# First mixture's weights in runs of 4 KB, and RWKV keys with the learning-rate factor left in PSUM

## The chip, the cores and the metric

One NeuronCore of a Trainium2 chip runs the whole program. The metric is the time of one execution on the device in microseconds. The kernel before took 2755.37 us (median of 3 runs, 2753.96 to 2766.93).

The engines: TensorE multiplies matrices (weights loaded first, then a matmul that streams the other operand) and writes to PSUM; VectorE, ScalarE and GpSimd work element by element, each on 128 partitions; the first two read and write SBUF and PSUM, GpSimd SBUF only. SyncE here only issues DMAs, in order, each behind a wait for what it needs. Every engine runs its own instructions in order.

## The reference

Two layers over 512 latent and 256 context tokens of 1024 channels, fp32. Layer 0 mixes tokens by neighbourhood attention, layer 1 by a bidirectional RWKV-7 scan; each is followed by a mixture of 16 experts in which every expert takes the 64 latent (in layer 0 also the 32 context) tokens with the highest affinity.

```
y   = segment_sum(((silu(xin @ w1) * (xin @ w3)) @ w2) * gate)      # per expert: [cap,1024] x [1024,1024], three times
kk  = k * k_k ; kk = kk / max(norm(kk per head), 1e-12)               # k = xk @ w_k
a_z = sigmoid(a0_z + (xa @ a1_z) @ a2_z)                              # learning rate, z = forward, backward
scan inputs: kk, kk * a_z, kt_z = k * (1 + (a_z - 1) * k_a), decay from w0, w1, w2
bonus = sum over z of sum per head(r * kt_z * r_k)
```

## The kernel before, in words

**Mixture.** For each expert twelve weight tiles of 1 MB ([128, 2, 1024] fp32) go through a ring of SBUF buffers (`load_weights`, L637): eight of `w1` and `w3` by turns, four of `w2`. A tile holds 256 rows of the matrix; partition p has rows 2p and 2p+1, one run of 8 KB (`"(p k) n -> p k n"`, L645). So a tile's half k holds every second row, and the activations that multiply it have to hold every second channel. `pair_cols` (L69) picks these columns when activations are turned with a transpose on TensorE (`transpose`, L75 to L77: the data is loaded as weights, the identity is multiplied): gathered tokens `xg` in `channels` (L659; used by `gather` and, for the router, by `route_tile` on `XN`), and the hidden rows `hid` and `hidc` in `expert` (L805, L814). The norm's gain, the adaLN columns and the router weights follow the same order of channels (`load_vectors`, `ada`, `moe_open`). TensorE computes `P` (L790, latent) and `Pc` (L795, context), then `w2` (L823, L828). A weight DMA is issued on SyncE's queue once TensorE has done with the tile that its buffer held.

**Keys.** `rw_inputs` weaves the products of layer 1 (`w_r`, `w_k`: L260 to L262, three passes per product) with `rw_keys`, which goes over four blocks of 256 channels (n), each in six steps of 128 tokens (t). `norms` multiplies k by `k_k` on GpSimd for a pair of steps (L1199), squares on ScalarE and sums on VectorE. `weights` loads two rows of vectors (`krows`, one buffer: the DMA waits until GpSimd has done with the block before) and the LoRA matrices, and splits these in high and low parts `w2s` and `w`. A step has three parts. `first`: GpSimd multiplies k by `k_k` again (`kkb`, L1232) and by half of `k_a` (`kr`, L1234); TensorE makes two PSUM tiles `mk` (L1241, L1242; three buffers), ScalarE takes tanh of them into SBUF, `sig` for the decay and `av` for the learning rate (L1243). `second`: `kkb` is normalised on VectorE (L1250), ScalarE makes `hk` from it, and VectorE makes `kka` (L1257) and in two operations the new `av` (L1259, L1260) from the factor; all go to DRAM (`pkd`). `third` (latent steps, four a block): GpSimd's three products and VectorE's sum `cf` for the bonus. After the last block come the value products (`xvh`, `xvl` from `xraw`; weights `w_v`, of which `wh` is made on ScalarE at L252 and `wl` on VectorE at L253).

**Order.** Each engine's order is made when the program is built, by a list scheduler that goes by simulated times and the priorities that the code gives. So an edit in one place can move instructions of others, on every engine and on the DMA queues.

Of the kernel before, what the change touches and what calls it, by code (L numbers as in the profile page):

```python
# [31 lines left out]
P = 128  # L32
# [36 lines left out]
def pair_cols(k):  # L69

    o = 2 * P * (k // 2)
    return slice(o + k % 2, o + 2 * P, 2)
# [7 lines left out]
def load_vectors(S):  # L80


    nc, cp, I = S.nc, S.cp, S.I
    cr = S.small.tile([16, P], F32, name="crows", bufs=1)
    nc.sync.dma_start(cr[0:8], I["c"].rearrange("o (k p) -> (o k) p", p=P))
    nc.sync.dma_start(cr[8:16], I["c_ctx"].rearrange("(k p) -> k p", p=P))
    S.sT = cp.tile([P, KD, 32], F32, name="sT")
    nc.vector.memset(S.sT, 0.0)
    pt = S.ps_tp.tile([P, 512], F32, name="tp")
    transpose(S, pt[:, :16], cr)  # L90
    nc.scalar.activation(S.sT[:, :, 0:2].rearrange("p k w -> p w k"),
                         pt[:, 0:16].rearrange("p (w k) -> p w k", w=2), AF.Silu)
    rows = S.small.tile([18, P], F32, name="rows", bufs=1)
    rows2 = S.small.tile([8, 2 * P], F32, name="rows2", bufs=1)
    q = nc.gpsimd
    q.dma_start(rows[0:16], I["norm1_g"].rearrange("l (k p) -> (l k) p", p=P))
    q.dma_start(rows2, I["norm2_g"].rearrange("l (k c) -> (l k) c", c=2 * P))
# [4 lines left out]
    transpose(S, pt[:, :18], rows)  # L102
    for s in range(2):
        transpose(S, pt[:, 18 + 8 * s:26 + 8 * s], rows2[:, s::2])
    S.vT = cp.tile([P, 34], F32, name="vT")
    nc.vector.tensor_copy(S.vT[:, 0:18], pt[:, 0:18])
    nc.vector.tensor_copy(S.vT[:, 18:34].rearrange("p (k s) -> p s k", s=2),
                          pt[:, 18:34].rearrange("p (s k) -> p s k", s=2))
    S.g1T = [S.vT[:, 8 * l:8 + 8 * l] for l in range(2)]
    S.g2T = [S.vT[:, 18 + 8 * l:26 + 8 * l] for l in range(2)]  # L110
    S.qgT = cp.tile([P, 1], F32, name="qgT")
    nc.vector.tensor_scalar(S.qgT, S.vT[:, 16:17], DH ** -0.5, None, op0=ALU.mult)
    S.kgT = S.vT[:, 17:18]
    S.modT = [cp.tile([P, 48, 2], F32, name=f"modT{l}") for l in range(2)]


def ada(S, l, j):
# [22 lines left out]
    for s in range(2):  # L140
        transpose(S, pt[:, s, :], acc[:, s::2] if j in (3, 4) else acc[:, s * P:(s + 1) * P])
# [459 lines left out]
def moe_open(S, l, es):  # L601
# [9 lines left out]
    if WRING[l][0]:  # L611
# [3 lines left out]
    nc.gpsimd.dma_start(R.wr.rearrange("p (k s) e -> p k (s e)", s=2),  # L615
                        I["moe_router"][l].rearrange("(k p s) e -> p k (s e)", p=P, s=2))
# [42 lines left out]
def channels(S, rows):  # L659
# [11 lines left out]
def route_tile(S, R, t):  # L671
# [14 lines left out]
    modulated(S, R, channels(S, XN), t // NLT, hT)  # L686
# [81 lines left out]
def gather(S, R, i, w):  # L768
# [3 lines left out]
    modulated(S, R, channels(S, xg), w, xin)  # L772
# [3 lines left out]
def expert(S, R, e, xin, xinc, wk, psh, Y, YC):  # L776
# [27 lines left out]
    for c in range(4):  # L804
        transpose(S, pt[:, c * P:(c + 1) * P], hid[:, pair_cols(c)])  # L805
    hT = wk.tile([P, 4, 2, CAPL], F32, name="hidT")
    nc.scalar.activation(hT.rearrange("p c h s -> p (c h s)"), pt, AF.Copy)  # L807
    if ctxs:
# [4 lines left out]
        for c in range(4):  # L813
            transpose(S, pt[:, c * 64:(c + 1) * 64], hc[0:64, pair_cols(c)])  # L814
# [350 lines left out]
SPREAD, LOQ, KSB, BOOST = 8, 7, 6, 1000  # L1165
# [7 lines left out]
def rw_keys(S, ready):  # L1173
# [15 lines left out]
    def norms(n, C):  # L1189
# [3 lines left out]
        C.ss = kp.tile([P, NT, 4], F32, name="kss")  # L1193
        for t in range(0, NT, 2):
# [751 lines left out]
```

## Time and profile before

| | |
|---|---|
| profiled execution | 2758.18 us |
| its span | 2756.4 us |
| TensorE busy | 2470.2 us (90%) |
| VectorE, ScalarE, GpSimd busy | 1327.1, 1004.0, 591.5 us |
| DMA | 637.64 MB, mean 231 GB/s |
| weight tiles of the mixtures | 378 on SyncE's queue, 6 on GpSimd's, 1024 KB each |

The span is the time from the first to the last instruction of the profiled execution, the rest of its own time lies around it. An instruction is named by its line in the program, engine, and out<-in by the program's names. A busy TensorE need not be at its peak: its clock is granted in two levels (1.2 and 2.4 GHz; 1.00 is the higher). "a <- b" in a list of waits says that a stood idle until b was done. Stages follow one another: attention to 640 us, the first mixture to 1283, RWKV inputs to 1388, keys to 1523, their tail to 1571, values and scan to 2232, and the second mixture.

### The profile page before, as it was taken

To read this page: it belongs to the slowest core of one execution; us is meant where nothing else is said; L and a number is where in the kernel's file an instruction comes from. 1 tells how busy PE (TensorE), PEld (TensorE's weight loads), DVE (VectorE), ACT (ScalarE), POOL (GpSimd) and SP (SyncE) were. 2 spreads that over 40 slices of the span, in tenths; PEclk is the share of its full clock that TensorE was granted. 3 is DMA by queue.
4 is the path that set the end of the run, shared out by engine and by line. 5 is a ranking of instruction groups with operands and counts; after the bars stand their busy time and mean duration, and the time that the engine had idled before them with its cause. 6 is when DMAs were issued, how large, how long until landed. Compare 5 with 4: busy or idle time off the path is not lost. (4 is left out here: it accounts for less than half of the span.)

```text
span 2756.4 us, 44025 instructions
## 1 busy us (share of the span) xinstructions
PE 2470.2 (90%) x16800; PEld 1574.1 (57%) x16800; DVE 1327.1 (48%) x3006; ACT 1004.0 (36%) x2127; POOL 591.5 (21%) x857
## 2 busy tenths in 40 slices
PE   6998999898999999997698697999999977998887
PEld 4876879793333333333388686777777862332222
DVE  6665566642222222225978845666666771221222
ACT  3555556642111101113266634766665431000100
POOL 2100000121000000001656525665655110000000
PEclk9999999998999999998899898999999978999999
DMA  8646440328787878784157866565554369999998
GB/s 246 147 150 187 132 152 15 109 100 327 298 320 312 334 305 329 293 357 172 69 186 241 269 167 130 124 134 125 126 122 125 87 243 378 420 420 421 420 420 342
DMA packets 378371, 637.64 MB, mean 231 GB/s; under 512 B 133832, under 2 KB 301056, under 8 KB 329008
## 3 DMA queue, kind: packets, MB, share of 16 engines
q1 hardware_dynamic: 370944, 609.11, 63.5%
q0 software_dynamic: 7216, 25.70, 2.5%
q8 instruction: 134, 2.20, 0.3%
q14 instruction: 77, 0.63, 0.1%
HBM read 565.11 MB, written 53.88 MB: 225 GB/s over the span
## 5 line engine op out<-in xcount | busy, mean ns | idle before, releaser
L790 PE MATMUL P<-wm,xin 128*64 128x512 f32 x2048 | 494.3, 601 | 25.8 <-DMA wm<-in_moe_w_dram 24.7
L790 PEld LDWEIGHTS P<-wm,xin 128*64 128x64 f32 x2048 | 141.0, 137 | 328.3 <-issue 259.4
L823 PE MATMUL mm<-wm,hidT 128*64 128x512 f32 x1024 | 245.9, 601 | 16.8 <-ACT hidT L807 14.9
L801 ACT ACTIVATE hid<-P 128x512 f32<-128x512 f32 x32 | 19.1, 597 | 563.3 <-PE P L790 563.3
L763 POOL DMA_INDIRECT xg<-xnd,ii x20 | 19.7, 985 | 846.5 <-PE tp L77 571.5
L837 DVE SCALAR_TENSOR_TENSOR Y<-mm,gates,gt 64x512 f32<-64x512 f32 x64 | 48.0, 750 | 283.1 <-PE mm L823 282.4
L260 PE MATMUL mm<-wh,hTh 128*128 128x256 f32 x576 | 173.5, 302 | 1.9 <-ACT hTh L554 1.9
L802 DVE TENSOR_TENSOR hid<-P,hid 128x512 f32<-128x512 f32 x32 | 22.1, 692 | 308.3 <-PE P L790 293.6
L262 PE MATMUL mm<-wh,hTl 128*128 128x256 f32 x576 | 168.4, 293 | 1.9 <-DVE hTl L557 1.9
L261 PE MATMUL mm<-wl,hTh 128*128 128x256 f32 x576 | 168.7, 293 | 0.0
L823 PEld LDWEIGHTS mm<-wm,hidT 128*64 128x64 f32 x1024 | 72.7, 137 | 151.9 <-issue 121.3
L1477 POOL TENSOR_TENSOR Wi<-Wi,Ti 112x30 f32<-112x30 f32 (+14 forms) x240 | 141.4, 589 | 18.8
L1475 POOL TENSOR_TENSOR Ti<-Wi 112x30 f32<-112x30 f32 (+14 forms) x240 | 134.9, 562 | 18.2
L795 PE MATMUL Pc<-wm,xin 128*32 128x512 f32 x1024 | 138.5, 597 | 0.0
L260 PEld LDWEIGHTS mm<-wh,hTh 128*128 128x128 f32 x576 | 114.3, 199 | 11.9 <-issue 8.8
L262 PEld LDWEIGHTS mm<-wh,hTl 128*128 128x128 f32 x576 | 113.6, 198 | 4.5 <-DVE hTl L557 2.8
L1554 PE MATMUL mm<-FR,QF 128*128 128x128 f32 (+1 forms) x768 | 115.1, 294 | 0.4 <-ACT QF L1542 0.4
L261 PEld LDWEIGHTS mm<-wl,hTh 128*128 128x128 f32 x576 | 114.6, 199 | 1.3 <-issue 1.1
L864 DVE TENSOR_TENSOR X<-mm,X 128x512 f32<-128x512 f32 x80 | 52.6, 687 | 111.9 <-PE mm L863 111.7
L1554 PEld LDWEIGHTS mm<-FR,QF 128*128 128x128 f32 x768 | 98.7, 200 | 7.4 <-ACT QF L1542 0.9
L1542 ACT ACTIVATE QF<-mm 64x256 f32<-64x256 f32 x192 | 72.6, 378 | 67.7 <-PE mm L1538 64.3
L1557 DVE TENSOR_TENSOR FT<-mm,eye 64x128 f32<-64x128 f32 x192 | 55.8, 292 | 78.9 <-ACT FT L1556 76.6
(437 smaller groups left out, 5715.6 us busy)
## 6 DMA issues: line engine op xcount, KB each, us to landing
wm<-in_moe_w_dram SPq DMA_DIRECT2D x378, 1024.0 KB
adaw<-in_ada_w_dram SPq DMA_DIRECT2D x96, 512.0 KB
wraw<-in_na_w_qkv_dram SPq DMA_DIRECT2D x32, 256.0 KB
wm<-in_moe_w_dram POOLq DMA_DIRECT2D x6, 1024.0 KB, 10.8
pkd<-sig SPq DMA_DIRECT2D x24, 256.0 KB
pkd<-kka SPq DMA_DIRECT2D x24, 256.0 KB
pkd<-av SPq DMA_DIRECT2D x24, 256.0 KB
sig<-pkd SPq DMA_DIRECT2D x16, 384.0 KB
```

Of the source, the lines that this page charges most:

```text
L260: S.nc.tensor.matmul(ps, xh, wh, start=(k == 0), stop=False)
L261: S.nc.tensor.matmul(ps, xh, wl, start=False, stop=False)
L262: S.nc.tensor.matmul(ps, xl, wh, start=False, stop=(k == n - 1))
L790: nc.tensor.matmul(ps[64 * hf:64 * hf + 64], xin[:, k, cl], w[:, hf * 512:(hf + 1) * 512], start=k == 0, stop=k == KD - 1)
L795: nc.tensor.matmul(Pc[32 * i:32 * i + 32], xinc[:, k, cc], ws[k][i // 2][:, (i % 2) * 512:(i % 2 + 1) * 512], start=k == 0, stop=k == KD - 1)
L823: nc.tensor.matmul(py[64 * hf:64 * hf + 64], hT[:, k % 4, k // 4, :], ws[k][:, hf * 512:(hf + 1) * 512], start=k == 0, stop=k == KD - 1)
L864: nc.vector.tensor_tensor(X[t][:, sl], ps, X[t][:, sl], op=ALU.add)
L1475: nc.gpsimd.tensor_tensor(t, W3[:, i + 1:32, i:i + 1].to_broadcast([112, n, i]), W3[:, i:i + 1, 0:i].to_broadcast([112, n, i]), op=ALU.mult)
L1477: nc.gpsimd.tensor_tensor(W3[:, i + 1:32, 0:i], W3[:, i + 1:32, 0:i], t, op=ALU.add)
L1542: nc.scalar.activation(QF[m][0:64, u], pq[64 * u:64 * u + 64], AF.Copy)
L1554: nc.tensor.matmul(pf[:, h, s0:], QF[m][:, u, h, :], rhs, start=True, stop=True)
L1557: nc.vector.tensor_tensor(F[64:128, :, 64:128], pf[64:128, :, 64:128], S.eye2[64:128, None, :].to_broadcast([64, 2, 64]), op=ALU.add)
```

## The change

In layer 0 alone, a weight tile's half k holds 128 neighbouring rows, so that each partition reads two runs of 4 KB; transposes, gain, adaLN columns and router weights of layer 0 go by neighbouring columns too. The second mixture stays with 8 KB. In the keys, `k * k_k` is made once for a pair of steps (`kkp`, four buffers, also the squares' source), and the learning-rate factor's tanh stays in its PSUM tile, from which VectorE's three operations read it; the last writes `av` to SBUF.

```diff
-def pair_cols(k):
+def block_cols(l, k):
+    if l == 0:
+        return slice(k * P, (k + 1) * P)
     o = 2 * P * (k // 2)
     return slice(o + k % 2, o + 2 * P, 2)
...
-    ...rearrange("(p k) n -> p k n", p=P))
+    ...rearrange(("(k p) n -> p k n", "(p k) n -> p k n")[R.l], p=P))
...
-            transpose(S, pt[:, i, :], rows[:, pair_cols(k)])
+            transpose(S, pt[:, i, :], rows[:, block_cols(l, k)])
...
-        transpose(S, pt[:, c * P:(c + 1) * P], hid[:, pair_cols(c)])
+        transpose(S, pt[:, c * P:(c + 1) * P], hid[:, block_cols(R.l, c)])
...
+            C.kp.append(kp.tile([P, 2, 256], F32, name="kkp", bufs=KPB))
+            q.tensor_tensor(C.kp[-1], k, both(C.kk), op=ALU.mult)
             sq = kp.tile([P, 2, 256], F32, name="kka")
-            q.tensor_tensor(sq, k, both(C.kk), op=ALU.mult)
-            nc.scalar.activation(sq, sq, AF.Square)
+            nc.scalar.activation(sq, C.kp[-1], AF.Square)
...
-        T.kk = kp.tile([P, 256], F32, name="kkb")
-        q.tensor_tensor(T.kk, T.k, C.kk, op=ALU.mult)
+        T.kk = C.kp[t // 2][:, t % 2, :]
...
-        T.av = kp.tile([P, 2, 256], F32, name="av", bufs=3)
-        for hid, i, dst in zip(S.hid, (0, 2), (T.sig, T.av)):
-            ps = S.ps_k.tile([P, 2, 256], F32, name="mk")
+        for hid, i in zip(S.hid, (0, 2)):
+            T.pa = ps = S.ps_k.tile([P, 2, 256], F32, name="mk")
...
-            nc.scalar.activation(dst, ps, AF.Tanh, scale=0.5)
+            nc.scalar.activation(ps if i else T.sig, ps, AF.Tanh, scale=0.5)
...
+        T.av = av = kp.tile([P, 2, 256], F32, name="av")
...
-        nc.vector.scalar_tensor_tensor(kka, av, 1.0, both(hk), op0=ALU.add, op1=ALU.mult)
+        nc.vector.scalar_tensor_tensor(kka, pa, 1.0, both(hk), op0=ALU.add, op1=ALU.mult)
...
-        nc.vector.scalar_tensor_tensor(av, av, -1.0, both(T.kr), op0=ALU.add, op1=ALU.mult)
-        nc.vector.tensor_tensor(av, av, both(T.k), op=ALU.add)
+        nc.vector.scalar_tensor_tensor(pa, pa, -1.0, both(T.kr), op0=ALU.add, op1=ALU.mult)
+        nc.vector.tensor_tensor(av, pa, both(T.k), op=ALU.add)
```

The order moves with it. SyncE's queue at the keys' tail, before (`r`, `av` and `krows` belong to the keys, `xraw` are the inputs of the value products; line numbers are each kernel's own):

```order
L1265 DMA r<-rd_10635 128x256
L955 DMA xraw<-xmd_10648 128x770
L955 DMA xraw<-xmd_10649 128x770
L955 DMA xraw<-xmd_10650 128x770
L955 DMA xraw<-xmd_10651 128x770
L955 DMA xraw<-xmd_10652 128x770
L955 DMA xraw<-xmd_10653 128x770
L955 DMA xraw<-xmd_10654 128x770
L955 DMA xraw<-xmd_10655 128x770
L1261 DMA pkd_10658<-av 128x2x256
L1170 DMA krows<-in_rw_k_a_dram 128x256
L1170 DMA krows<-in_rw_r_k_dram 128x256
```

The same place now:

```order
L1273 DMA r<-rd_10636 128x256 x2
L1177 DMA krows<-in_rw_k_a_dram 128x256
L1177 DMA krows<-in_rw_r_k_dram 128x256
L1269 DMA pkd_10659<-av 128x2x256
L1263 DMA pkd_10659<-sig 128x2x256
L962 DMA xraw<-xmd_10649 128x770
L962 DMA xraw<-xmd_10650 128x770
L962 DMA xraw<-xmd_10651 128x770
L962 DMA xraw<-xmd_10652 128x770
L962 DMA xraw<-xmd_10653 128x770
```

The last block's `krows` now go ahead of the eight `xraw`, which stand behind a store of `av` and one of `sig`.

TensorE in the last block, the second pair of `mk` tiles of a step before (`hs` and `h` are the LoRA activations of either direction, the last two numbers apart):

```order
L1241 MATMUL mk<-w2s,hs_10731 128x256 [waits Activation_49]
L1242 MATMUL mk<-w_13031,h_10732 128x256
L1241 MATMUL mk<-w2s,hs_10733 128x256
L1242 MATMUL mk<-w_13031,h_10734 128x256
L1241 MATMUL mk<-w2s,hs_10727 128x256 [waits Activation_49]
```

The same place now:

```order
L1248 MATMUL mk<-w2s,hs_10732 128x256 [waits DVE_49]
L1249 MATMUL mk<-w_13007,h_10733 128x256
L1248 MATMUL mk<-w2s,hs_10734 128x256
L1249 MATMUL mk<-w_13007,h_10735 128x256
L1248 MATMUL mk<-w2s,hs_10728 128x256 [waits Activation_49]
```

The first matmul into a reused `mk` tile waited for ScalarE and now, in 21 groups of the program (2 before), for VectorE.

## Rows read from the trace of the kernel before

**Rows 1.** The page's view of stages, asked for four stretches (first mixture, keys, keys' tail, second mixture): start and end in us, length, busy us and number of instructions of TensorE (PE), its weight loads (PEld), VectorE (DVE), ScalarE (ACT) and GpSimd (POOL), the granted TensorE clock, the DMA engines' busy share, GB/s.

```profile
640.00:1283.00 643.00, 632.42 (x3937) 224.71 (x3933) 143.44 (x246) 80.78 (x175) 10.44 (x15) 1.00 0.78 316
1388.00:1523.00 135.00, 124.39 (x998) 122.16 (x996) 103.60 (x126) 89.05 (x154) 83.65 (x82) 0.97 0.70 221
1523.00:1571.00 48.00, 25.24 (x131) 21.73 (x130) 41.55 (x54) 30.81 (x50) 29.27 (x30) 0.72 0.89 292
2310.00:2757.00 447.00, 391.49 (x1708) 136.31 (x1704) 97.70 (x162) 38.35 (x75) 5.62 (x6) 0.99 0.98 408
```

**Rows 2.** Who waited for whom, TensorE in the first mixture (640 to 1283 us), longest in total first: us in total, times, longest.

```profile
PE mm L823 <- ACT hidT L807: 7.9, 11, 0.7
```

**Rows 3.** The same for SyncE's DMA queue, same stretch.

```profile
SPq L645 <- PE Pc L795: 335.9, 75, 40.3
```

**Rows 4.** Stages again: two stretches with the DMA engines full, one where nearly all runs are of 4 KB (adaLN and attention weights), one where the weights of the first mixture come in 8 KB runs.

```profile
12.00:16.00 4.00, 2.09 (x16) 0.43 (x16) 0.75 (x2) 3.07 (x6) 0.00 (x0) 1.00 1.01 367
640.00:704.00 64.00, 62.63 (x372) 18.47 (x370) 6.18 (x10) 8.13 (x16) 1.97 (x2) 1.00 1.01 419
```

**Rows 5.** Transposes (L77), the weight loads: name, number, shortest/median/longest in ns, first and last start in us, shapes. `sb` is read in neighbouring columns, `xg` in every second one.

```profile
L77 PEld LDWEIGHTS tp<-ident,sb x320: 137/140/231, 101.5 to 530.2; 128*128 128x128 f32 x160
...
L77 PEld LDWEIGHTS tp<-ident,xg x160: 193/208/227, 634.5 to 2677.6; 128*128 128x128 f32 x160
```

**Rows 6.** TensorE in order of time, in the attention, around a block of four transposes of neighbouring columns: start in us, us, line, operation, number merged.

```profile
107.62 0.66 PE L77 MATMUL tp<-ident,sb 128*128 128x128 f32 x4
108.21 0.66 PE L406 MATMUL po<-PT,V 128*64 128x128 f32 x8
```

**Rows 7.** The same in the first mixture, around a block of four transposes of every second column.

```profile
713.89 0.75 PE L77 MATMUL tp<-ident,xg 128*128 128x128 f32 x4
714.57 0.65 PE L790 MATMUL P<-wm,xin 128*64 128x512 f32 x2
```

**Rows 8.** Who waited for whom, TensorE in the keys and their tail (1380 to 1570 us).

```profile
PE mk L1242 <- DVE w L1226: 7.2, 1, 7.2
```

**Rows 9.** GpSimd by line, keys and tail (1380 to 1571 us): number | busy us, mean ns | idle us before, by whom it was ended.

```profile
L1232 POOL TENSOR_TENSOR kkb<-ks,rowk 128x256 f32<-128x256 f32 x24 | 23.2, 973 | 29.8 <-ACT hk L1253 18.7 <-DMA pkd<-kkb 11.1
```

**Rows 10.** VectorE by line, same stretch.

```profile
L1259 DVE SCALAR_TENSOR_TENSOR av<-av,kr 128x512 f32<-128x512 f32 x24 | 22.1, 928 | 4.9 <-POOL kr L1234 4.7
L1260 DVE TENSOR_TENSOR av<-av,ks 128x512 f32<-128x512 f32 x24 | 22.1, 923 | 0.2
L1257 DVE SCALAR_TENSOR_TENSOR kka<-av,hk 128x512 f32<-128x512 f32 x24 | 20.9, 870 | 5.8 <-ACT av L1243 4.4 <-ACT hk L1253 1.2
```

**Rows 11.** Two lines of VectorE over the whole execution: number, shortest/median/longest in ns. L1257 reads two operands from SBUF, L305 (attention) one from PSUM and one from SBUF.

```profile
L1257 DVE SCALAR_TENSOR_TENSOR kka<-av,hk x24: 675/693/1231, 1408.0 to 1568.9; 128x512 f32<-128x512 f32 x24
...
L305 DVE TENSOR_TENSOR sq<-mm,qrs x24: 671/684/692, 69.0 to 496.9; 128x512 f32<-128x512 f32 x24
```

**Rows 12.** ScalarE in order of time: the second tanh of the ninth, eleventh and seventeenth step.

```profile
1464.16 0.59 ACT L1243 ACTIVATE av<-mk 128x512 f32<-128x512 f32 x1
...
1474.68 0.59 ACT L1243 ACTIVATE av<-mk 128x512 f32<-128x512 f32 x1
...
1517.21 0.59 ACT L1243 ACTIVATE av<-mk 128x512 f32<-128x512 f32 x1
```

**Rows 13.** VectorE in order of time: the last operation on the factor in the ninth, fifteenth and nineteenth step (the nineteenth is the first of the last block of heads).

```profile
1475.95 1.12 DVE L1260 TENSOR_TENSOR av<-av,ks 128x512 f32<-128x512 f32 x1
...
1517.61 1.12 DVE L1260 TENSOR_TENSOR av<-av,ks 128x512 f32<-128x512 f32 x1
...
1545.58 1.23 DVE L1260 TENSOR_TENSOR av<-av,ks 128x512 f32<-128x512 f32 x1
```

**Rows 14.** SyncE's queue in order of time, tail.

```profile
1524.69 3.98 SPq L955 DMA_DIRECT2D xraw<-xmd  x8
1531.05 0.37 SPq L1261 DMA_DIRECT2D pkd<-av  x1
1531.52 0.53 SPq L1170 DMA_DIRECT2D krows<-in_rw_k_a_dram  x1
...
1546.08 0.62 SPq L273 DMA_DIRECT2D wraw<-in_rw_w_v_dram  x1
```

**Rows 15.** ScalarE in order of time, tail.

```profile
1541.14 0.42 ACT L1211 ACTIVATE krows<-krows 128x256 f32<-128x256 f32 x1
...
1552.05 1.06 ACT L252 ACTIVATE wh<-wraw 128x1024 fp32r<-128x1024 f32 x1
...
1559.51 0.42 ACT L1253 ACTIVATE hk<-kkb 128x256 f32<-128x256 f32 x1 [4.64 <-DVE kkb L1250]
...
1561.97 1.04 ACT L252 ACTIVATE wh<-wraw 128x1024 fp32r<-128x1024 f32 x1
```

**Rows 16.** GpSimd in order of time, tail.

```profile
1541.64 2.32 POOL L1234 TENSOR_TENSOR kr<-ks,krows 128x256 f32<-128x256 f32 x2 [11.55 <-ACT krows L1211]
```

**Rows 17.** TensorE in order of time, tail.

```profile
1553.16 1.01 PE L260 MATMUL mm<-wh,xvh 128*128 128x256 f32 x3 [0.60 <-ACT wh L252]
...
1563.07 0.62 PE L260 MATMUL mm<-wh,xvh 128*128 128x256 f32 x3 [1.48 <-ACT wh L252]
1563.55 1.56 PE L1332 MATMUL un<-sig,tri 128*128 128x512 f32 x4
1566.60 0.39 PE L261 MATMUL mm<-wl,xvh 128*128 128x256 f32 x1 [1.49 <-DVE wl L253]
```

More of the change, by code (lines that the diff above doesn't have):

```diff
@@ L92, in load_vectors @@
                          pt[:, 0:16].rearrange("p (w k) -> p w k", w=2), AF.Silu)
-    rows = S.small.tile([18, P], F32, name="rows", bufs=1)
-    rows2 = S.small.tile([8, 2 * P], F32, name="rows2", bufs=1)
+    rows = S.small.tile([26, P], F32, name="rows", bufs=1)
+    rows2 = S.small.tile([4, 2 * P], F32, name="rows2", bufs=1)
     q = nc.gpsimd
     q.dma_start(rows[0:16], I["norm1_g"].rearrange("l (k p) -> (l k) p", p=P))
-    q.dma_start(rows2, I["norm2_g"].rearrange("l (k c) -> (l k) c", c=2 * P))
+    q.dma_start(rows[18:26], I["norm2_g"][0].rearrange("(k p) -> k p", p=P))
+    q.dma_start(rows2, I["norm2_g"][1].rearrange("(k c) -> k c", c=2 * P))
     for i, n in enumerate(("na_q_g", "na_k_g")):
@@ L101, in load_vectors @@
     pt = S.ps_tp.tile([P, 512], F32, name="tp")
-    transpose(S, pt[:, :18], rows)
+    transpose(S, pt[:, :26], rows)
     for s in range(2):
-        transpose(S, pt[:, 18 + 8 * s:26 + 8 * s], rows2[:, s::2])
+        transpose(S, pt[:, 26 + 4 * s:30 + 4 * s], rows2[:, s::2])
     S.vT = cp.tile([P, 34], F32, name="vT")
-    nc.vector.tensor_copy(S.vT[:, 0:18], pt[:, 0:18])
-    nc.vector.tensor_copy(S.vT[:, 18:34].rearrange("p (k s) -> p s k", s=2),
-                          pt[:, 18:34].rearrange("p (s k) -> p s k", s=2))
+    nc.vector.tensor_copy(S.vT[:, 0:26], pt[:, 0:26])
+    nc.vector.tensor_copy(S.vT[:, 26:34].rearrange("p (k s) -> p s k", s=2),
+                          pt[:, 26:34].rearrange("p (s k) -> p s k", s=2))
     S.g1T = [S.vT[:, 8 * l:8 + 8 * l] for l in range(2)]
@@ L140, in ada @@
     for s in range(2):
-        transpose(S, pt[:, s, :], acc[:, s::2] if j in (3, 4) else acc[:, s * P:(s + 1) * P])
+        transpose(S, pt[:, s, :], acc[:, s::2] if l == 1 and j in (3, 4) else acc[:, s * P:(s + 1) * P])
     nc.vector.tensor_copy(S.modT[l][:, 8 * j:8 * j + 8, :].rearrange("p (q s) w -> p s q w", s=2),
@@ L614, in moe_open @@
     R.wr = R.pool.tile([P, KD, E], F32, name="wr")
-    nc.gpsimd.dma_start(R.wr.rearrange("p (k s) e -> p k (s e)", s=2),
-                        I["moe_router"][l].rearrange("(k p s) e -> p k (s e)", p=P, s=2))
+    if l == 0:
+        nc.gpsimd.dma_start(R.wr, I["moe_router"][l].rearrange("(k p) e -> p k e", p=P))
+    else:
+        nc.gpsimd.dma_start(R.wr.rearrange("p (k s) e -> p k (s e)", s=2),
+                            I["moe_router"][l].rearrange("(k p s) e -> p k (s e)", p=P, s=2))
     R.trow = R.pool.tile([P, 512], F32, name="trow")
@@ L656, in modulated, with channels @@
         S.nc.scalar.activation(dst[:, k], src(k), AF.Identity, scale=a[:, k:k + 1], bias=b[:, k:k + 1])
-def channels(S, rows):
+def channels(S, l, rows):
     pts = []
@@ L813, in expert @@
         for c in range(4):
-            transpose(S, pt[:, c * 64:(c + 1) * 64], hc[0:64, pair_cols(c)])
+            transpose(S, pt[:, c * 64:(c + 1) * 64], hc[0:64, block_cols(R.l, c)])
         hTc = wk.tile([P, 4, 2, CAPC], F32, name="hidTc")
@@ L1164 @@
 MXB = {"mx": 5, "md": 2}
-SPREAD, LOQ, KSB, BOOST = 8, 7, 6, 1000
+SPREAD, LOQ, KSB, BOOST, KPB = 8, 7, 6, 1000, 4
 KSTART, KRATE = 0, 1.75
@@ L1193, in norms @@
         C.ss = kp.tile([P, NT, 4], F32, name="kss")
+        C.kp = []
         for t in range(0, NT, 2):
@@ L1242, in first @@
                 nc.tensor.matmul(ps[:, z, :], h1, C.w1[:, i + z, :], start=False, stop=True)
-            nc.scalar.activation(dst, ps, AF.Tanh, scale=0.5)
+            nc.scalar.activation(ps if i else T.sig, ps, AF.Tanh, scale=0.5)
         return T
     def second(n, t, C, T):
-        sig, av = T.sig, T.av
+        sig, pa = T.sig, T.pa
+        T.av = av = kp.tile([P, 2, 256], F32, name="av")
         out = S.pk[n][t * P:(t + 1) * P]
```

6 lines of the change are left out of this document (3 added, 3 removed).

## The prediction

> **What bounds the kernel now.** The table of windows by stage comes first, since the change sits in two stages only [rows 1]. The first mixture (640 to 1283 us) has TensorE busy for 632.42 of 643 us at full clock while the DMA engines are busy 0.78 of the time: TensorE bounds it, and the weight stream has slack. The RWKV keys (1388 to 1523 us) have TensorE busy for 124.39 of 135 us; VectorE (103.60) and GpSimd (83.65) run close behind. Then comes a stretch I call the keys' tail (1523 to 1571 us), where TensorE works 25.24 of 48 us at a mean clock of 0.72: nothing on TensorE bounds it, a chain over four engines and the DMA does. The second mixture is bound by its weights (DMA share 0.98) and the change leaves it as it is.
>
> The waits come second. In the first mixture TensorE waits 7.9 us for `hidT`, and no weight is named [rows 2]; the weight queue waits 335.9 us for TensorE to release tiles of the ring [rows 3], so the ring is full. In the keys TensorE's longest wait is one of 7.2 us for the last block's `w` [rows 8]; the timelines of that place are read under the tail.
>
> **First mixture, run length.** Each weight tile (1.05 MB) is now read as two 4 KB runs a partition where it was one of 8 KB. The trace has 4 KB runs at the start of the program, when only these stream: 367 GB/s at a share of 1.01 (12 to 16 us), against 419 at 1.01 for 8 KB runs [rows 4]. The stage needs 192 tiles, 201.3 MB; at 367 GB/s that is 549 us, some 90 us under the 643 us of TensorE. So the stage's DMA share rises from 0.78 to about 0.88 and its time stays: 0 us. The cover is the slack of 94 us; it would be gone if the rate fell under 201.3 MB / 643 us = 313 GB/s.
>
> **First mixture, transposes.** In layer 0 the transposes read 128 neighbouring columns rather than every second one. The weight load of a transpose of every second column (`xg`) takes 208 ns, of neighbouring columns (`sb`) 140 ns [rows 5]. How much of these 68 ns TensorE sees is read from starts: a block of four `xg` is followed 0.68 us later by the next instruction (713.89 to 714.57) [rows 7], a block of four `sb` between matmuls of 64 columns 0.59 us later (107.62 to 108.21) [rows 6]. That is 0.09 us a block. The stage has 24 blocks of `xg`, 16 of `hid` and 16 of `hidc`: and the last, of half the height, I count at half: 40 x 0.09 + 16 x 0.045 = 4.3 us, all of it on the bound engine. From below 1 us (only some blocks follow work that hides no load), from above 224 x 68 ns = 15 us (no load hidden at all). I take 4.5, since the pairs of starts measure just this.
>
> The Trainium skill speaks against this term: its page "SBUF — State Buffer", section "Door 1: The DMA port swizzle", says that SBUF is read in lines of 16 bytes and that fp32 may be strided by up to four elements for free. By that rule the term is 0 and the sum 4.5 us poorer. The loads of 208 and 140 ns at the same size [rows 5] do not agree with it, and I go by them.
>
> **Keys, main part.** GpSimd loses 24 multiplications of 973 ns, 23.2 us of its 83.65 [rows 1, 9]. VectorE's three operations on the learning-rate factor (mean 870, 928 and 923 ns [rows 10]) read one operand from PSUM instead of SBUF. What that costs the trace shows in L305, a product of a PSUM and an SBUF operand of the same size: 671 to 692 ns [rows 11], so nothing is added. Yet none of this is on the bound engine; what reaches the end is only TensorE's idle time here, 135 - 124.4 = 10.6 us [rows 1].
>
> Against it stands a new wait. The factor's PSUM tile is no longer free once ScalarE has read it, but only after VectorE's last operation on it; with three tiles in turn, TensorE's matmuls for the factor of step t+2 wait for VectorE to finish step t (21 groups of matmuls now wait for VectorE, 2 did before). Behind a waiting group stand the products of `w_r` and `w_k`, in order. In the trace VectorE ended the ninth step's last operation at 1475.95 + 1.12 = 1477.07 us [rows 13], while the matmuls for the eleventh step were done before ScalarE read them at 1474.68 [rows 12]: with the old timing TensorE would have stood there for about 2.5 us. The fifteenth step ended at 1517.61 + 1.12, the seventeenth's matmuls were read at 1517.21: 1.5 us. At the other steps VectorE was done first, so 4 us in all. VectorE and GpSimd with less to do shorten this lag. So: from -6 (over half of the 10.6 us idle goes) to +10 (four or five such stalls); I take +1, near the 4 us at the old lags less some relief.
>
> **Keys, tail.** On SyncE's queue the last block's rows `krows` stood behind eight loads of `xraw`: issued at 1531.52, the eight having begun at 1524.69 [rows 14]. ScalarE could scale them only at 1541.14 [rows 15], and GpSimd stood idle for 11.55 us until 1541.64 [rows 16]. Now `krows` stands ahead of the eight. That wait goes, but not all it held: the eight loads now stand behind the stores of the fifth `av` and sixth `sig` of the block before, which I put at about 1528 (the fifth `av` was stored at 1531.05 [rows 14], and VectorE now does it before two operations on `w` that came ahead of it), and ScalarE makes four `xvh` from them before the first tanh. So the first step's `av` ends about 3 us sooner (some 1543.5 for 1546.8 [rows 13]), not 11. The first half of `w_v`, issued behind it, goes out 1 or 2 us sooner than 1546.08 [rows 14], but its `wh` on ScalarE is now behind the fifth step's tanh: about 1554 for 1552.05. TensorE thus starts the values as late as before (1553.16 [rows 17]). What goes is the second stop: the second `wh` was made at 1561.97, behind a wait of ScalarE of 4.64 us for `kkb`, which VectorE had late from GpSimd [rows 15], and TensorE stood from 1561.6 to 1566.60 but for 1.56 us of other matmuls [rows 17]. With the steps no longer waiting for GpSimd the second `wh` comes at about 1558, its low part 3.5 us later (as 1566.60 follows 1563.07 [rows 17]), by when the first half's products end: 5.0 - 1.6 = 3.4 us saved. With what the clock gives back I take -4. Bounds: -9 (the whole of both stops in rows 17 and the two times between) and +4 (the first `wh` late by 2 us more, and the old stop still there).
>
> **Elsewhere** the order moves by single places (attention, the start, the scan); the one added 4 KB vector load at the start lies beside the adaLN stream. 0, by +-2.
>
> **Sum.** -4.5 + 1 - 4 = -7.5 us. The profiled execution took 2758.2 us, 2.8 above the median of the runs shown (2755.4): 2750.7 on its own terms, 2747.9 beside the median. I predict 2748 us, a gain of 0.3%. Less than 0.5% (13.8 us) is what a measurement of this kernel cannot tell from no change.
>
> **Rivals.**
> *Relief.* VectorE's operations on two SBUF operands take 675 to 1231 ns (`kka`) [rows 11], the long ones beside GpSimd, with means of 870 to 928 [rows 10]; those with a PSUM operand, at 671 to 692, show no such spread [rows 11]. If the three operations fall to 685 ns even beside GpSimd, VectorE gains 24 x (0.870 + 0.928 + 0.923 - 3 x 0.685) = 16.0 us and GpSimd as much beside its 23.2; then the main part gives 6 and the tail 9: -4.5 - 6 - 9 = -19.5, 2736 us. Against it: L305 ran where GpSimd was mostly idle, and the bound engine has only 10.6 us to give.
> The Trainium skill has this as a rule: "SBUF — State Buffer", section "Who interferes with whom", says that a VectorE instruction with at most one SBUF input does not contend with GpSimd, one with two does. No row here shows it for PSUM beside a busy GpSimd; it leans towards this rival.
> *Nothing arrives.* The loads of transposes turn out hidden and the tail waits for `xraw` and `w_v` as long as before (the DMA share there is 0.89 [rows 1]): 0 to -2, 2754 us.
> *Slower: TensorE stalls for PSUM tiles.* Place: the groups that now wait for VectorE; price: the lag of VectorE behind the tanh (12.9 us for the ninth step, 1464.16 to 1477.07 [rows 12, 13]) less what TensorE has in front. Two steps are 2 x 135/24 = 11 us; once the lag stays over that, each of some 12 groups costs 2 us and the clock falls: +24 - 4.5 = 2775 us. It decides from a lag of 11 us on average; in the trace it is over 11 in some steps only, and the work of both engines shrinks.
> *Slower: 4 KB runs bind the mixture.* At 300 GB/s it would take 671 us, +28, 2776 us; 367 at the start speaks against it [rows 4].
>
> **How the numbers follow.** The forecast 0.52 (own range 2738 to 2758), relief 0.24, nothing 0.12, stalls 0.10, 4 KB runs 0.02. Faster by over 0.5% (under 2741.6): three quarters of relief and a fifth of the forecast, 0.28. Slower by over 0.5% (over 2769): two thirds of both slow cases and a little for orders that I haven't followed, 0.10. Range: 2730 (relief with most of the 15 us of loads) to 2765 (half of the stalls).
>
> **What would show it.** First mixture: loads of `xg` and `hid` near 140 ns, a stage some 4 us shorter, DMA share 0.85 to 0.9, no wait on `wm`. Main part: no `kkb` on GpSimd, waits `mk <- DVE` of 0 to 4 us in all, TensorE busy about 124 us of a stage within 3 us of 135. Tail: no wait of `kr` on `krows` over 3 us, first value matmul at 1553 +-3 on a shifted clock, no second stop. I am wrong if `mk` waits for VectorE by over 10 us, if a weight tile is waited for in the first mixture, or if transposes still load in 200 ns.

## The result, and the profile after

The changed kernel takes 2734.28 us (median of 4 executions, 2732.44 to 2736.23), the kernel before on the same chip 2758.4 (4, 2753.96 to 2766.93; the prediction reckoned from the 2755.4 of three of them): a ratio of 0.9907, with an interval of 0.9883 to 0.9931. The time lies inside the predicted range of 2730 to 2765, 13.7 us under the predicted 2748; the gain is more than the 0.5% under which I had expected to find it. The profiled execution took 2732.64 us. From its page, the span and TensorE's busy time:

```profile
span 2730.8 us, 43954 instructions
...
PE 2455.0 (90%) x16800; PEld 1554.1 (57%) x16800; DVE 1298.9 (48%) x3006; ACT 1005.4 (37%) x2127; POOL 561.5 (21%) x834
...
DMA packets 402978, 637.63 MB, mean 233 GB/s; under 512 B 133860, under 2 KB 301088, under 8 KB 378192
```

TensorE is busy for 15 us less than before (2470.2) with no product gone. The packets are 24,607 more than the 378,371 of the page before, which is the second run of each partition: 192 tiles x 128 = 24,576.

The stages of [rows 1] in the changed kernel (first mixture, keys, tail, second mixture; each window lies where the stage now lies):

```profile
632.00:1271.00 639.00, 627.93 (x3943) 216.27 (x3939) 143.23 (x246) 80.88 (x175) 11.71 (x17) 1.00 0.82 318
1376.00:1507.00 131.00, 123.39 (x986) 121.08 (x985) 84.72 (x129) 89.33 (x154) 62.66 (x67) 0.97 0.72 229
1507.00:1555.00 48.00, 29.31 (x152) 25.37 (x153) 33.17 (x53) 28.31 (x45) 19.27 (x22) 0.64 0.91 307
2284.00:2731.00 447.00, 393.05 (x1710) 137.06 (x1706) 97.72 (x162) 38.38 (x75) 5.63 (x6) 0.99 0.98 408
```

The first mixture is 4 us shorter by this window, with a DMA share of 0.82 after 0.78. In the keys VectorE is busy for 84.72 us (103.60 before) and GpSimd for 62.66 (83.65). The second mixture is what it was.

Windows cut by eye are too coarse for a few us, so each trace was also cut at the same six marks of TensorE's timeline: the first expert matmul, the first transpose of layer 1's inputs, the last `w_r`/`w_k` product, the last `w_v` product, the last transpose of the scan's output, the end. Control and after again are repeats of the two kernels (below). In us, worked out from those times, to about half a us:

| | before | control | moe only | keys only | after | after again |
|---|---|---|---|---|---|---|
| attention, to first expert | 636.4 | 632.0 | 632.2 | 631.1 | 628.8 | 630.3 |
| first mixture | 654.7 | 656.5 | 649.9 | 656.3 | 650.5 | 650.3 |
| keys, main part | 232.2 | 232.0 | 238.0 | 227.0 | 227.3 | 227.9 |
| tail and value products | 141.7 | 145.1 | 142.5 | 139.8 | 138.4 | 140.2 |
| scan | 567.2 | 563.9 | 571.5 | 571.8 | 561.7 | 562.8 |
| second mixture and end | 524.3 | 525.2 | 525.2 | 524.4 | 524.2 | 521.2 |

Mean of the two traces of before against mean of the two of after: mixture -5.2, keys -4.5, tail -4.1, attention -4.7, scan -3.3, end -2.1; together -23.8. The first three are where the change acts; the last three are taken up below.

### The profile page after: what moved, and what is told of

Same layout as the page of the kernel before. It is cut to its first block, busy times and chain, and to the rows that moved or that the text cites. A ratio compares the mean times of both kernels' runs of the same rounds, so it can differ in the third digit from the quotient of the medians.

```text
span 2730.8 us, 43954 instructions
## 1 busy us (share of the span) xinstructions
PE 2455.0 (90%) x16800; PEld 1554.1 (57%) x16800; DVE 1298.9 (48%) x3006; ACT 1005.4 (37%) x2127; POOL 561.5 (21%) x834
## 5 line engine op out<-in xcount | busy, mean ns | idle before, releaser
L797 PEld LDWEIGHTS P<-wm,xin 128*64 128x64 f32 x2048 | 141.7, 137 | 327.5 <-issue 266.3
```

Of the source, the lines that this page charges most:

```text
L797: nc.tensor.matmul(ps[64 * hf:64 * hf + 64], xin[:, k, cl], w[:, hf * 512:(hf + 1) * 512], start=k == 0, stop=k == KD - 1)
```

## The experiments

Twelve runs, each timed beside the kernel before on the same chip; the chips differ between runs, so ratios are compared and not medians. Ratios are against it, with their 95% intervals; the control has one execution and no ratio.

| run | ratio | interval | median us |
|---|---|---|---|
| control | | | 2756.46 |
| moe_only | 0.9965 | 0.9951 to 0.9979 | 2750.71 |
| keys_only | 0.9962 | 0.9946 to 0.9977 | 2746.39 |
| psum_only | 0.9967 | 0.9948 to 0.9987 | 2747.87 |
| kkp_only | 0.9994 | 0.9977 to 1.0011 | 2756.13 |
| after_again | 0.9922 | 0.9895 to 0.9948 | 2734.15 |
| runs4k_strided | 1.0003 | 0.9989 to 1.0016 | 2757.47 |
| runs8k_blocks | 0.9978 | 0.9963 to 0.9994 | 2753.12 |
| five_slots | 0.9947 | 0.9929 to 0.9965 | 2744.08 |
| two_slots | 0.9957 | 0.9941 to 0.9973 | 2746.03 |
| krows2k3 | 0.9921 | 0.9900 to 0.9942 | 2735.39 |
| xraw_queue | 0.9917 | 0.9897 to 0.9937 | 2736.88 |

### The two kernels again

No edit. The kernel before, once more:

> The kernel before, unchanged, traced once more to see how much its stages scatter. Theory A (scatter): the attention (until the first expert's matmul, 636.4 us in the trace of before, 628.8 in that of the changed kernel) starts or ends several us away from 636.4 in this trace too, by its waits for the adaLN weights (11.2 us in 9 waits before, 6.0 in 5 changed). Theory B (order): it stays within 1 us of 636.4, and the 7.6 us belong to the changed order. The mixture and the keys stay within 1 us of their lengths in both.

And the changed one:

> The changed kernel once more, for its ratio with more runs and a second trace of its stages. The parts alone gave 0.9965 (mixture) and 0.9962 (keys); if they add, 0.993; if the 0.9907 of four runs holds, the two orders made together gain some 6 us that neither part has.

The attention took 632.0 us in the control, where the first trace had 636.4; it lies between 631.1 and 633.2 in the other traces without the whole change and between 628.4 and 631.3 in those of after and its variants. So some 4 us of the 7.6 between the first two traces are scatter of executions. The kernel before ran 29 times beside these experiments, between 2747.44 and 2768.77 us: single executions differ by more than most parts of the change are worth, and a stage of one trace shows little under 3 us.

### The mixture's half and the keys' half

All hunks outside `rw_keys`, of which this one sets the order of the channels:

```diff
-def pair_cols(k):
+def block_cols(l, k):
+    if l == 0:
+        return slice(k * P, (k + 1) * P)
```

> The first mixture's part alone (4 KB runs, transposes of neighbouring columns), the keys as before. Theory of the prediction: loads of xg and hid at 140 ns, the mixture (first to last expert matmul) 4 to 5 us shorter than before, keys unchanged; total -4 to -5 us, ratio about 0.998. If the attention's 7.6 us belong to this part's other start (one more vector load) it is -12, ratio 0.9955.

All hunks inside it:

```diff
-        T.kk = kp.tile([P, 256], F32, name="kkb")
-        q.tensor_tensor(T.kk, T.k, C.kk, op=ALU.mult)
+        T.kk = C.kp[t // 2][:, t % 2, :]
...
-            nc.scalar.activation(dst, ps, AF.Tanh, scale=0.5)
+            nc.scalar.activation(ps if i else T.sig, ps, AF.Tanh, scale=0.5)
```

> The keys' part alone (k times weights made once, factor in PSUM), first mixture as before. Theory 1 (relief): keys and their tail give some 8 us and the scan behind them 5 to 6, as in the changed kernel: -14 us, ratio 0.995; VectorE's three operations at 680 to 700 ns with none over 750. Theory 2 (the scan's gain came from another order that the first mixture's part brought): -8 us, ratio 0.997.

Each half is worth about a third of a per cent and they multiply: 0.9965 x 0.9962 = 0.9927, beside the 0.9922 of both together. The first mixture is 649.9 us with the one half and 656.3 with the other, so its gain belongs to the mixture's half alone. The keys' main part and tail shorten with the keys' half (227.0 and 139.8). Its ratio lies between the two theories and decides neither; its one trace shows no gain in the scan (571.8). That moe_only's profile has 238.0 for a main part whose code it leaves alone I can't explain; its order there moved too, and runs8k_blocks, which differs from it only in the run length, has some 236.

### Run length or transposes

The next two kernels don't compute the layer, since rows of the weights meet the wrong channels; they are there for their times. In the first only the weights' runs become 4 KB; the activations keep every second column:

```diff
-    ...rearrange("(p k) n -> p k n", p=P))
+    ...rearrange(("(k p) n -> p k n", "(p k) n -> p k n")[R.l], p=P))
```

> The kernel before with 4 KB runs in the first mixture and nothing else: activations keep every second column, so rows of the weights meet the wrong channels and the output is not the reference's; every instruction keeps its size. Theory 1 (only the transposes count): mixture 655 to 657 us as before, loads of xg and hid at 208 ns, DMA share about 0.8 to 0.85, ratio 1.000 +- 0.002. Theory 2 (the run length itself helps or hurts): the mixture moves by 3 us or more.

The reverse, the neighbouring columns with the 8 KB runs kept (the mixture's half without the line above):

> The first mixture's part without the 4 KB runs: transposes, gains and router weights go by neighbouring columns, the weights stay in 8 KB runs, so rows of the weights meet the wrong channels and the output is not the reference's. Theory 1: the mixture is 6 us shorter as in moe_only (650 us), loads of xg and hid at 140 ns, ratio 0.9965 to 0.998. Theory 2 (the run length): mixture 656 us.

The page's view of stages, first of runs4k_strided, then of runs8k_blocks:

```profile
636.00:1279.00 643.00, 633.22 (x3940) 224.96 (x3937) 142.64 (x244) 80.90 (x175) 10.87 (x16) 1.00 0.81 316
```

```profile
636.00:1272.00 636.00, 625.67 (x3935) 215.64 (x3931) 141.90 (x240) 80.78 (x175) 10.34 (x15) 1.00 0.79 319
```

By the marks the mixture takes 656.4 us with 4 KB runs alone and 650.0 with the columns alone. Over all fourteen traces the six with every second column lie between 654.7 and 656.5 (mean 656.0) and those with neighbouring ones between 649.3 and 650.5 (mean 650.2). So the mixture's gain is 5.8 us, all of it from the columns; the run length does nothing, as the prediction has it. These 5.8 us are 0.21%, as in the ratio of runs8k_blocks (0.9978); the 0.35% of moe_only are more, but the two intervals overlap, and what else that half may give is not shown. The weight loads show the rest. Transposes in the first mixture by line, before: count, then busy us and mean ns:

```profile
L77 PEld LDWEIGHTS tp<-ident,xg 128*128 128x128 f32 x88 | 13.7, 204 | 7.0 <-issue 6.1
L77 PEld LDWEIGHTS tp<-ident,hid 128*128 128x128 f32 x64 | 8.9, 208 | 13.4 <-issue 10.9 <-DVE pm L853 2.5
L77 PEld LDWEIGHTS tp<-ident,hidc 64*128 64x128 f32 x64 | 8.8, 209 | 13.0 <-issue 13.0
```

and after:

```profile
L80 PEld LDWEIGHTS tp<-ident,xg 128*128 128x128 f32 x88 | 10.4, 140 | 7.7 <-issue 6.1
L80 PEld LDWEIGHTS tp<-ident,hid 128*128 128x128 f32 x64 | 6.7, 141 | 13.4 <-issue 10.9 <-DVE pm L860 2.5
L80 PEld LDWEIGHTS tp<-ident,hidc 64*128 64x128 f32 x64 | 5.2, 138 | 13.0 <-issue 13.0
```

A load of `hidc` has half the rows of one of `xg` or `hid` and takes as long: 209 ns, now 138. What TensorE sees of it is in its order of time, before:

```profile
665.80 0.69 PE L77 MATMUL tp<-ident,hidc 64*128 64x64 f32 x4
666.42 1.94 PE L823 MATMUL mm<-wm,hidT 128*64 128x512 f32 x8
```

and after:

```profile
698.48 0.46 PE L80 MATMUL tp<-ident,hidc 64*128 64x64 f32 x4
698.87 0.66 PE L80 MATMUL tp<-ident,xg 128*128 128x128 f32 x4
...
706.92 0.66 PE L80 MATMUL tp<-ident,xg 128*128 128x128 f32 x4
707.51 1.94 PE L797 MATMUL P<-wm,xin 128*64 128x512 f32 x8
```

From start to next start such a block of `xg` falls from 0.68 us [rows 7] to 0.59, as worked out, and one of `hidc` from 0.62 to 0.39. Sixteen of the latter give 16 x 0.23 = 3.7 us. Summed in this way over all blocks of the stage in the traces of before and after, `hidc` gives 3.7 us, `xg` 1.2 and `hid` 0.8: 5.6 of the 5.8 us.

### The keys' two edits apart

The factor stays in PSUM, `kkb` stays as it was:

```diff
-        for hid, i, dst in zip(S.hid, (0, 2), (T.sig, T.av)):
-            ps = S.ps_k.tile([P, 2, 256], F32, name="mk")
+        for hid, i in zip(S.hid, (0, 2)):
+            T.pa = ps = S.ps_k.tile([P, 2, 256], F32, name="mk")
```

> Only the factor stays in PSUM; the products of k and the weights are made twice, as before, so GpSimd keeps its 24 multiplications (23 us). If relief by the PSUM operand is what helps: VectorE's three operations at 680 to 700 ns beside a GpSimd that is as busy as before, and at least half of the keys' gain: -4 to -8 us against before. If it is the work taken from GpSimd: the three operations spread up to 1.2 us as before, and 0 to -2 us, or slower by the waits for PSUM tiles.

`k * k_k` is made once (with three buffers), the factor goes to SBUF as before:

```diff
+            C.kp.append(kp.tile([P, 2, 256], F32, name="kkp", bufs=KPB))
+            q.tensor_tensor(C.kp[-1], k, both(C.kk), op=ALU.mult)
...
-        T.kk = kp.tile([P, 256], F32, name="kkb")
-        q.tensor_tensor(T.kk, T.k, C.kk, op=ALU.mult)
+        T.kk = C.kp[t // 2][:, t % 2, :]
```

> Only k times weights made once (three buffers for it instead of four, since the factor's third SBUF buffer is still there); the factor stays in SBUF. GpSimd loses its 24 multiplications of 973 ns. If the PSUM operand makes the gain: VectorE's three operations still spread to 1.2 us with means over 800 ns, and the ratio is 0.999 to 1.001. If GpSimd's work makes it: means under 750 ns and a ratio of 0.996 to 0.998.

By the ratios, leaving the factor in PSUM gives as much as the keys' half (0.9967 beside 0.9962 for both edits); kkp_only can't be told from no change. VectorE's three operations by line in keys and tail (count, busy us, mean ns, idle before), kkp_only:

```profile
L1258 DVE SCALAR_TENSOR_TENSOR kka<-av,hk 128x512 f32<-128x512 f32 x24 | 20.3, 846 | 5.2 <-DMA pkd<-kka 4.1 <-ACT hk L1254 1.0
L1260 DVE SCALAR_TENSOR_TENSOR av<-av,kr 128x512 f32<-128x512 f32 x24 | 20.1, 845 | 5.1 <-POOL kr L1235 4.6
L1261 DVE TENSOR_TENSOR av<-av,ks 128x512 f32<-128x512 f32 x24 | 19.6, 825 | 0.3
```

and the changed kernel:

```profile
L1267 DVE SCALAR_TENSOR_TENSOR mk<-mk,kr 128x512 f32<-128x512 f32 x24 | 16.6, 693 | 1.7 <-POOL kr L1242 1.6
L1265 DVE SCALAR_TENSOR_TENSOR kka<-mk,hk 128x512 f32<-128x512 f32 x24 | 16.5, 686 | 9.3 <-ACT mk L1250 4.5 <-DMA pkd<-kka 4.0 <-DMA pkd<-av 0.8
L1268 DVE TENSOR_TENSOR av<-mk,ks 128x512 f32<-128x512 f32 x24 | 16.4, 686 | 2.3 <-DMA pkd<-av 2.0
```

With one multiplication of GpSimd less they fall from 870 to 928 ns [rows 10] to 825 to 846; with an operand in PSUM to 686 to 693, and in psum_only, beside a GpSimd that has all its work, to 683 to 691. GpSimd gains as well, in psum_only by line:

```profile
L1232 POOL TENSOR_TENSOR kkb<-ks,rowk 128x256 f32<-128x256 f32 x24 | 20.4, 853 | 23.9 <-DMA pkd<-kkb 20.4 <-ACT mk L1242 3.2 <-ACT hk L1253 0.2
L1234 POOL TENSOR_TENSOR kr<-ks,krows 128x256 f32<-128x256 f32 x24 | 18.7, 786 | 15.0 <-ACT krows L1211 14.3 <-DVE cf L1269 0.6
```

`kkb` took 973 ns before [rows 9]. This is the relief of the rival, on both engines, at the 685 ns that it named. The other edit relieves VectorE in a place that the rival did not count, the normalisation of `kkb` or `kkp`. Control, then the changed kernel:

```profile
L1250 DVE TENSOR_TENSOR kkb<-kkb,kss 128x256 f32<-128x256 f32 x24 | 16.6, 708 | 4.7 <-POOL kkb L1232 4.5
L1258 DVE TENSOR_TENSOR kkp<-kkp,kss 128x256 f32<-128x256 f32 x24 | 9.5, 456 | 0.2
```

It takes 419 ns in kkp_only and 761 in psum_only, so this relief of 7 us belongs to the product that is made once.

Where psum_only's 0.33% (9 us) lies is not settled: in its one profile the main part is 230.7 us, the tail 143.1 and the scan 556.6, so most of it stands in the scan, whose code it leaves alone. By the marks kkp_only has some 230 and 143 us too. In these traces, then, each edit alone takes 1 to 2 us from the main part and next to nothing from the tail, and both together (keys_only) 5 and 4: the stages do not show that one edit carries the half.

### How many PSUM tiles

In the changed kernel the decay's matmuls go to the two tiles of the transposes' pool, so that the factor has three to itself:

```diff
-            T.pa = ps = S.ps_k.tile([P, 2, 256], F32, name="mk")
+            if i:
+                T.pa = ps = S.ps_k.tile([P, 2, 256], F32, name="mk")
+            else:
+                ps = S.ps_tp.tile([P, 512], F32, name="tp").rearrange("p (z c) -> p z c", z=2)
```

> The changed kernel, with the decay's matmuls in the two PSUM buffers of the transposes (idle in the keys) and the three buffers left to the factor, so that TensorE waits for VectorE's end of step t only at step t+3. Theory (the new wait costs what the trace shows): the waits of mk for VectorE, 9.8 us in keys and tail, fall under 4 us, and the time falls by 2 to 6 us against the changed kernel (ratio to before 0.990 against 0.992). Rival (other waits take their place, since VectorE, ScalarE and the stores pace the steps): waits of mk for others grow by as much, and the time is the changed kernel's within 2 us.

And one tile taken from the three:

```diff
-    S.ps_k = S.rwk.enter_context(tc.tile_pool(name="ps_k", bufs=3, space=PSUM))
+    S.ps_k = S.rwk.enter_context(tc.tile_pool(name="ps_k", bufs=2, space=PSUM))
```

> The changed kernel with two PSUM buffers for mk instead of three: a tile for the factor then waits for VectorE's end of the step before. The rival of the prediction, that TensorE stalls for PSUM tiles, made large on purpose: each of 24 steps waits for a lag of VectorE of some 3 to 10 us, less what stands ahead: 24 x 1 to 3 us, so waits of mk for VectorE and ScalarE of 30 to 70 us and a kernel at 0.998 to 1.015 of before. If it stays under 0.995, the number of tiles never was a threat.

Who waited for whom, TensorE in keys and tail (us in total, times, longest), in five_slots and in two_slots:

```profile
PE mm L264 <- ACT wh L256: 16.8, 3, 13.4
PE mk L1251 <- DVE av L1271: 8.7, 5, 2.5
```

```profile
PE mk L1248 <- ACT sig L1250: 10.6, 6, 3.9
PE mk L1248 <- DVE av L1268: 5.4, 3, 4.1
```

By the ratios more tiles came out slower than the changed kernel (0.9947 beside 0.9922, intervals that overlap a little). In the main part the wait for VectorE falls to 1.2 us, but the part gets no shorter (229 us). The rest of the 8.7 us stands in the tail, where the first value product now waits up to 13.4 us for `wh`, which the new order puts late on ScalarE (the tail takes 145.4 us); so neither theory held, and the run doesn't isolate the wait. One tile fewer costs some 10 us against the changed kernel by the ratios (0.9957 beside 0.9922, intervals that overlap a little too) and is still faster than the kernel before, where I had expected 0.998 or more. Where these 10 us lie isn't shown: in its one trace, an execution of 2739.10 us, the main part and the tail are as long as in the changed kernel (some 228 and 139 us). So three tiles are far from the point at which their number would decide; what the new wait costs by itself is not shown.

### The tail's two stops

In the changed kernel a second buffer for `krows`, paid for with one of `kkp`:

```diff
-        C.rows = kp.tile([P, 2, 256], F32, name="krows", bufs=1)
+        C.rows = kp.tile([P, 2, 256], F32, name="krows", bufs=2)
```

> The changed kernel with two buffers for krows (a block's rows load without waiting for GpSimd's end of the block before) and, for room, three instead of four for kkp. Theory (the tail is held by the chain from krows): GpSimd's wait for krows, 5.4 us in the tail of the changed kernel, goes, and the values start 1 to 4 us sooner after the end of the products. Rival: the tail is held by the eight loads of xraw, the tanh behind their copies, and stores; then GpSimd waits less and nothing else moves, within 2 us.

And the eight `xraw` on GpSimd's DMA queue instead of SyncE's:

```diff
-        S.nc.sync.dma_start(t, S.xmd[i][k])
+        (S.nc.gpsimd if tag == "xraw" else S.nc.sync).dma_start(t, S.xmd[i][k])
```

> The changed kernel with the eight loads of xraw issued on GpSimd's queue, where they no longer stand behind the stores of the last block but one, and with two instead of four copies xvh ahead of the last block's first tanh. If these hold the tail (in the changed kernel ScalarE waits 1.9 us for xraw and TensorE 4.3 us for the first tanh): TensorE's wait for that tanh falls under 2 us, the first value matmul comes 2 to 5 us sooner after the end of the products (32 us in the changed kernel), ratio to before about 0.991. Rival (the stores of kka and sig and w_v's load pace the tail): the first value matmul stays at 30 to 33 us after the products, ratio as the changed kernel's 0.992 or 0.993.

GpSimd's waits for `krows` (13.9 us in keys and tail of the changed kernel) are gone in krows2k3, and the time is the same (0.9921 beside 0.9922). With `xraw` on the other queue TensorE waits less for the first tanh of the last block but more for a later one. TensorE in order of time, changed kernel:

```profile
1521.87 0.58 PE L1248 MATMUL mk<-w2s,hs 128*128 128x256 f32 x1 [4.28 <-ACT sig L1250]
```

and xraw_queue:

```profile
1518.60 0.58 PE L1248 MATMUL mk<-w2s,hs 128*128 128x256 f32 x1 [1.43 <-ACT sig L1250]
...
1530.26 0.58 PE L1248 MATMUL mk<-w2s,hs 128*128 128x256 f32 x1 [3.09 <-ACT sig L1250]
```

In all, its waits for a tanh are 7.2 us after 7.1. Its first value product still starts 32.2 us after the last of the products before (31.9 in the changed kernel, 29.9 and 31.8 in the two traces of before), behind a wait of 3.8 us for `wh`, 1.8 in the changed kernel. Neither stop decides when the values start, and neither version beats the changed kernel.

## Why the prediction was right or wrong

**Sign and size.** Faster was right, and the range held. The sum of -7.5 us was short by two terms that the runs show, some 7 us, and by a remainder of about 10 that they don't place. So the place inside the range is in part luck: the time lies under the forecast's own 2738 to 2758 and beside the 2736 of the rival of relief, but the stages that this rival counts gave 14.4 us (5.8, 4.5, 4.1) and not its 19.5. That less than 0.5% can't be told from no change was too careful: with 12 executions the 0.35% of moe_only can be told (0.9951 to 0.9979).

**Run length, 0.** Right: 656.4 us with it alone. The DMA share rose to 0.82 (0.81 for the runs alone), under the 0.88 that I got from the rate at the start of the program, and no weight was waited for. The rival of 4 KB runs is out.

**Transposes, -4.5.** Right in kind, mis-sized: -5.8. The step that failed is "the last, of half the height, I count at half". A `hidc` load is as long as a full one, and its matmul streams 64 columns for 128; its block gave 0.23 us, not 0.045, so 3.7 us for 0.7. The other two kinds gave less than the sum has: `xg` 1.2 us for 24 x 0.09 = 2.2, with 0.09 only in some of its blocks and about 0.03 in others, and `hid` 0.8 for 1.4, since TensorE mostly waits there for `hidT` (8.5 us after, 7.9 before [rows 2]) and a shorter load only lengthens that wait. The rival on which nothing arrives is out. The rule of the Trainium skill that I set against this term ("SBUF — State Buffer", section "Door 1: The DMA port swizzle") gives 0 here; the 208 and 140 ns of the loads and the 5.8 us don't agree with it.

**Keys, main part, +1.** Wrong in sign: -4.5. Waits of TensorE in keys and tail, control (by line and releaser: us, times, longest) and then the changed kernel:

```profile
PE mk L1241 <- ACT w2s L1221: 10.5, 3, 4.0
PE mk L1242 <- DVE w L1226: 7.0, 1, 7.0
...
PE mm L261 <- DVE wl L253: 4.6, 4, 1.5
```

```profile
PE mk L1248 <- DVE av L1268: 9.8, 6, 2.5
...
PE mk L1249 <- DVE w L1235: 3.5, 1, 3.5
...
PE mk L1248 <- ACT w2s L1230: 1.7, 1, 1.7
```

The new wait is there: 4.8 us of the 9.8 fall into the main part, beside "4 us in all"; the 5 us in the tail stood in no term, and the sign of 0 to 4 us was missed. The step that failed is that I set only this wait into the sum and put the relief down as something that might shorten it. VectorE is 18.9 us less busy in this stage [rows 1], and TensorE waits less where a block starts: for `w2s` 10.5 us in the control and 6.7 in the trace of before, 1.7 in the changed kernel and 2.3 in its repeat; for `wl` 4.6 and 6.6, then under 1. The wait for the last block's `w` (7.0, and 7.2 in [rows 8]) falls to 3.5, but lies in the tail. That the relief ends these waits is argued, not shown; either edit alone shortens that for `w2s` (3.7 us in kkp_only, 1.1 in psum_only), and the longest for `w` is 7.4 in kkp_only, 3.5 in psum_only. On the other side waits for `ks` came in the main part (3.9 and 5.8 us in the two traces of after, 1.1 and none before). The rival of relief, at -6, was nearer than the forecast. The rule that stood behind it in the Trainium skill ("SBUF — State Buffer", section "Who interferes with whom") agrees with the rows here: at most one SBUF input, 686 to 693 ns beside GpSimd; two, 825 to 928. Against that rival I had put that TensorE has only 10.6 us of idle time to give; it gave 3 of them in the window of the profile (131 - 123.4 = 7.6 are left). The other 1.5 us of the 4.5 lie in its busy time and aren't explained. The rival of stalls for PSUM tiles is out: even with two tiles the kernel is faster than before.

**Keys, tail, -4.** The sum came out (143.4 to 139.3 on the means of two traces each, -4.1, with 2 to 3 us of scatter), and the steps mostly as told. SyncE's queue at the place of [rows 14], changed kernel:

```profile
1507.83 0.42 SPq L1177 DMA_DIRECT2D krows<-in_rw_k_a_dram  x1
...
1508.83 0.38 SPq L1269 DMA_DIRECT2D pkd<-av  x1
1509.25 0.47 SPq L1263 DMA_DIRECT2D pkd<-sig  x1
1509.89 5.81 SPq L962 DMA_DIRECT2D xraw<-xmd  x8
...
1530.95 0.40 SPq L277 DMA_DIRECT2D wraw<-in_rw_w_v_dram  x1
```

ScalarE there, to be set beside [rows 15], and GpSimd beside [rows 16]:

```profile
1537.42 1.06 ACT L256 ACTIVATE wh<-wraw 128x1024 fp32r<-128x1024 f32 x1 [0.98 <-DMA wraw<-in_rw_w_v_dram]
...
1542.64 1.06 ACT L256 ACTIVATE wh<-wraw 128x1024 fp32r<-128x1024 f32 x1 [0.67 <-DMA wraw<-in_rw_w_v_dram]
```

```profile
1511.91 1.50 POOL L1242 TENSOR_TENSOR kr<-ks,krows 128x256 f32<-128x256 f32 x2 [5.45 <-ACT krows L1220]
```

TensorE, to be set beside [rows 17]:

```profile
1538.53 1.00 PE L264 MATMUL mm<-wh,xvh 128*128 128x256 f32 x3 [1.84 <-ACT wh L256]
...
1540.83 0.41 PE L265 MATMUL mm<-wl,xvh 128*128 128x256 f32 x1
```

The products before end 16.6 us earlier than in the trace of before (1553.16 - 29.9 against 1538.53 - 31.9), so these starts are moved by that. The eight `xraw` go out at 1509.89, by the old clock 1526.5 (told: about 1528). The first `wh` comes at 1554.0 (told 1554), the first value product at 1555.2 (told 1553, give or take 3), the second `wh` at 1559.3 (told 1558), and from 1540.83 on TensorE runs without a stop through the second half: the second stop is gone. GpSimd's wait for `krows` is 5.45 us where I had said at most 3, and `w_v` goes out at 1547.6 by the old clock, later than 1546.08 and not sooner. Neither is worth anything by itself, as krows2k3 and xraw_queue show: the tail's gain lies behind the first value product. From there to the last one TensorE stood idle 9.8 and 10.0 us in the two traces of before, 4.6 and 5.3 in those of after. The second stop is 3.0 us of that (1.48 and 1.49 in [rows 17]; told 3.4); a wait for the first half's `wl` (1.95 and 1.44 us) went with it, which the sum did not have, and later stops changed places. The clock gave nothing back: 0.64 in the tail's window, 0.72 before.

**Elsewhere, 0 by +-2.** Not settled. Attention, scan and end together are 10 us shorter on the means of two traces. Some 4 us of the attention are the first trace's own scatter; without that trace its means are 629.9 us with the whole change (six traces) and 632.2 without (seven). Over all fourteen traces the scan takes 556.6 to 571.8 us in kernels that don't change its code, the same kernel agreeing within 1.1 to 3.3 us; so the order that the scheduler makes there may be worth as much as the change; that is a guess, as no run here took the scan's order by itself.

## What to carry to other kernels

Before putting a new wait into a sum alone, ask which waits of the same engine the relieved engines end: here waits of 9.8 us came and over 10 us of others went. An operation that is paid for in loads is to be read for each of its shapes, since one of half the size may take as long and be covered by less. And a stop on the way to a late start, such as the one for `krows`, may be worth nothing while something else comes as late, in xraw_queue the weights `wh`.

## What the hardware showed that I had not expected

The transposes' weight loads of half height and every second column took 209 ns, no less than full ones of 208, and a block of four gained 0.23 us from neighbouring columns where one of full height gained 0.09. Taking one SBUF operand from VectorE sped GpSimd up too: `kr` took 1033 and 1002 ns on average in the two traces of the kernel before, 786 in psum_only and 914 in kkp_only. And executions of one kernel on one chip spread over 21 us (2747.44 to 2768.77 for the kernel before), so that four of them can lie within 4 us or within 13.
